# An encoder layer on one core: the first down phase is put in another order, and the output weights change queues

## The chip, the core and the metric

The kernel is one program on one core of a Trainium2 chip. The number that counts is the device time of the whole program in microseconds, median over several executions. The engines are called as the profile calls them: PE (TensorE, matrix products), PEld (its weight loads), DVE (VectorE), ACT (ScalarE), POOL (GpSimd) and SP (SyncE, which here does little but issue transfers). Each engine works through its own instructions in the order in which they are written. A transfer is issued by an engine, mostly SP, and an issue that has to wait holds up whatever stands behind it on that engine.

## The reference

One layer of a hybrid encoder runs over a prompt of 2048 rows and, with caches, over a sample of 32 rows. Cut to what matters:

```python
proj  = x @ w_in                                     # q, k, v, forget logits, gates, h
mixed = concat([attention(q, k, v, logf), gate_b * causal_conv(gate_c * h)]) @ w_out
x = layer_norm(ALPHA * x + mixed)
g, val = split(x @ w_up)                             # 2 x 2816 columns
a = silu(causal_conv(g)) * val
x = layer_norm(ALPHA * x + a @ w_down)               # 2816 -> 1024
```

The last product, `a @ w_down`, is where most of the change lies, and the one with `w_out` where the rest does.

## The kernel before

All large products are made of three matmuls (`three`, L89 to L91): each factor is split into a rounded high part (`hi`, L80 on ACT or L78 on POOL) and the rest (`lo`, L85, a subtraction on DVE), and high x high, high x low and low x high are added up in PSUM. So each 128x512 piece of a weight needs a transfer, an ACT cast and a DVE subtraction before PE can use it.

The program has these stages, by the times of the trace: input projections and attention to about 1083 us; the output projection `mix` with its LayerNorm to 1310; then, for the first half of the prompt rows together with the sample rows, the products with `w_up` (`up(0)`, to 1757) and with `w_down` (`down(0)`, to about 2015); then `up(1)` (to about 2447) and `down(1)` for the other half. The products of a phase follow Strassen's scheme with seven products in place of eight. In a down phase these are p2, p1, p5, p6, p3, p7, p4, in this order; each has 11 steps k = 0 to 10, and a step is 12 matmuls of 512 columns (four tiles times `three`), called d0 to d10 below.

**Weight parts.** A generator, `left()`, makes the parts of all weights in the order of the PE's steps. A raw weight is loaded by SP into a tile `wr` (four of them), then split into a part `wp` (a ring of nine; a step of a down phase takes two). `steps()` gives the order for a down phase: the list of `("d", g, p, k)`, with the 22 sample steps `("s", f)` put in between. A sample step multiplies a 128-row block of `w_down` with the sample's rows (four matmuls, `sample`, L1339). Its moving side is `sm`, split from one table `VM` that is written to memory row by row in the up phase (`vm<-row`) and loaded back once, before the first sample step, when the up phase has issued all its transfers (`gated`). Of a sample step's weight the second half's low part is made on POOL (L1086), the first half's on DVE.

**Weight sums.** Four of the seven products need sums of blocks of `w_down`. `weight_sums(x)` (L1215, 22 calls) loads four blocks into a tile `yx`, adds them on POOL and stores them to `TW` (`tw<-yx`) some steps later. There is one call at the end of each turn f = 1 to 22 of `up(0)`.

**The next factors.** While `down(0)` runs p1 and later products, `build()` makes the prompt factors of `up(1)`: for each of four k it loads a tile `r` (one buffer) and two tiles `q` (two buffers) from `XT`, makes four differences on POOL (L912) and seven splits (ACT and DVE, tiles `xb` and `xt`). `free(k)` advances it by one piece after each step.

**The output weights.** `fetch_out` loads `w_out` in eight blocks `wor` (two buffers). The first three are split by POOL and DVE (`wh`, `wl`) during the stage before and issued by SP. The other five are split by ACT and DVE (`woh`, `wol`), and their loads are issued by ACT. In `mix`, `load` brings the attention's result back: `m<-mxs` for the sample, then `m<-mx` for the first tiles of the prompt, all issued by ACT; POOL casts them (`ms`, `mh`) and DVE subtracts (`ms`, `ml`).

The order within each engine is the order of the written program, adjusted by a scheduler, so that where an instruction ends up is read from the compiled order.

Of the kernel before, what the change touches and what calls it, by code (L numbers as in the profile page):

```python
# [7 lines left out]
F32 = mybir.dt.float32  # L8
# [3 lines left out]
ALU = mybir.AluOpType  # L12
# [10 lines left out]
GT = 512  # L23
FF = 2816
NF = 22
# [36 lines left out]
class Kernel:  # L62
# [141 lines left out]
    def fetch_out(self, upto, tiles=None):  # L204

        for k in range(len(self.out), upto):
            r = self.wp.tile([128, 4, 264], F32, tag="wr", bufs=2, name="wor").rearrange("p a b -> p (a b)")[:, :DM]
            if tiles:
                a, b = tiles(k)
            else:  # L210
                a, b = (self.wp.tile([128, 1152], F32R, tag=t, bufs=3, name=t)[:, :DM] for t in ("wh", "wl"))
            self.dma(r, self.i["w_out"][128 * k:128 * k + 128], self.nc.scalar if tiles else None)
            self.hi(a, r, "act" if tiles else "pool")
            self.lo(b, r, a)
            self.out.append((a, b))
# [686 lines left out]
    def build(self):  # L902

        for k in range(4):
            r = self.fp.tile([128, 1060], F32, tag="z", bufs=1, name="r")[:, :2 * GT].rearrange("p (r c) -> p r c", r=2)
            q = [self.fp.tile([128, 4, 128], F32, tag="s", bufs=2, name="q").rearrange("p a b -> p (a b)")
                 for _ in range(2)]
            self.dma(r, self.XT[k])
            for x in range(2):
                self.dma(q[x], self.XT[k + 4][:, x])  # L910
            yield
            sub = lambda o, x, y: self.nc.gpsimd.tensor_tensor(out=o, in0=x, in1=y, op=ALU.subtract)  # L912
            b11, b12, b21, b22 = r[:, 0], r[:, 1], q[0], q[1]
            src = {"b11": b11, "b21": b21, "b22": b22, "t1": b11, "t3": b12, "t2": b22, "t4": b21}
            todo = {"t1": (b12, b11), "t3": (b22, b12), "t2": (b22, b11), "t4": (b21, b22)}
            for s in self.SETS:
                if s in todo:
                    sub(src[s], *todo[s])
                self.split([self.X[s][1][:, x, k] for x in range(2)], src[s])
                yield  # L920
# [4 lines left out]
    def steps(self, g):  # L925

        out = []
        sample = iter(range(NF if g == 0 else 0))
        for p in self.DOWN:
            for k in range(NK):  # L930
                out.append(("d", g, p, k))
                for _, f in list(zip(range((0, 3, 3, 3, 3, 2)[min(k, 5)]), sample)):
                    out.append(("s", f))
        return out

# [14 lines left out]
    def left(self):  # L950


        nc = self.nc
# [77 lines left out]
        for p, v in (("p1", a11), ("p2", a12)):  # L1031
            w = as_part(self.rp.tile([128, DM], F32R, tag="wr", bufs=4, name="w" + p))
# [10 lines left out]
        for g in range(2):  # L1043
            for f in range(NF + 1):
                todo = ["p1", "p6", "p5", "p2", "p7"] if f else ["p1", "p2", "p5", "p6", "p7"]
                if g == 0 and f == 0:
                    todo = todo[3:]
                elif f < NF:
                    while ("u", g, f) not in R:
                        yield  # L1050
                    yield 1
                    item(g, f, todo.pop(0))
                if f:
                    for p in ("p4", "p3"):
                        yield 1
                        item(g, f - 1, p)
                    R.pop(("u", g, f - 1))
                    S.pop((g, f - 1))
                    more(2)
                if f < NF:  # L1060
                    for p in todo:
                        yield 1
                        item(g, f, p)
            if g == 0:
                sm, self.gated = [], False
            for key in self.steps(g):
                if key[0] == "s" and not len(sm):

                    while not self.gated:
                        yield  # L1070
                    m = raw()[:, :NF * TS].rearrange("p (f c) -> p f c", f=NF)
                    self.dma(m, self.VM)
                    for q in range(2):
                        v = self.fp.tile([128, DM], F32R, tag="yx", bufs=2, name="sm")[:, :NK * 2 * TS]
                        v = v.rearrange("p (f x c) -> p f x c", f=NK, x=2)
                        self.split([v[:, :, 0], v[:, :, 1]], m[:, NK * q:NK * q + NK])
                        sm += [v[:, f] for f in range(NK)]
                yield 2
                r = R.pop(key)
                parts = []  # L1080
                for h in range(2):
                    v = part().rearrange("p x a b -> p x (a b)")
                    w = r[:, GT * h:GT * h + GT]
                    if key[0] == "s" and h:
                        self.hi(v[:, 0], w, "act")
                        nc.gpsimd.tensor_tensor(out=v[:, 1], in0=w, in1=v[:, 0].bitcast(F32), op=ALU.subtract)  # L1086
                    else:
                        self.split([v[:, 0], v[:, 1]], w)
                    parts.append(v)
                self.W[key] = (sm[key[1]], parts) if key[0] == "s" else parts  # L1090
                more(1)
# [9 lines left out]
    def up(self, g, eb, pp, starts=()):  # L1101
        nc = self.nc
# [148 lines left out]
        for f in range(NF + 1):  # L1251
            steps = []
            if f < NF:
                steps.append(lambda: p1(f))
            if f:
                steps += [lambda: p4(f - 1), lambda: p3(f - 1)]
            late = f == 0
            if f < NF:
                steps += [lambda: p2(f)] if late else [lambda: p6(f)]
            if f:  # L1260
                steps.append(lambda: taps(f - 1))
            if f < NF:
                steps.append(lambda: p5(f))
            if f:
                steps.append(lambda: gate(f - 1))
            if f < NF:
                steps += [lambda: p6(f)] if late else [lambda: p2(f)]
            if f:
                steps.append(lambda: close(f - 1))
            if f < NF:  # L1270
                steps.append(lambda: p7(f))
            for s in steps:
                s()
                if starts:
                    starts.pop(0)()
                for x in later:
                    x[0] -= 1
                for x in [x for x in later if not x[0]]:
                    later.remove(x)
                    x[1]()  # L1280
                self.refill()
            if g == 0 and 0 < f:
                weight_sums(f - 1)
        for x in later:
            x[1]()
        self.gated = True
# [5 lines left out]
    def down(self, g, sb, pp):  # L1292
        nc = self.nc
# [3 lines left out]
        y = {}  # L1297
# [45 lines left out]
        def product(p, s, start, each, head=0, tail=0):  # L1343
            if start:
                self.K[s] = banks()

            def add(q, k):
                v, w = self.W["d", g, p, k]
                qs = slice(128 * q, 128 * q + 128)
                self.three(self.K[s][q], v[:, 0, qs], v[:, 1, qs], w[:, 0], w[:, 1],  # L1350
                           start and k == 0, k == NK - 1, skip_group_check=not start)

            def free(k):
                self.W.pop(("d", g, p, k))
                self.held -= 2
                self.refill()
                work()
                if p != "p2":
                    next(build, None)

            for q in range(4):
                for k in range(head):
                    add(q, k)
            for k in range(NK - tail):
                if k >= head:
                    for q in range(4):
                        add(q, k)
                if k >= head - 1:
                    for x in range(head if k == head - 1 else 1):
                        free(k - (head - 1 - x) if k == head - 1 else k)  # L1370
                        if p == "p2" and g == 0:
                            while [w for w in self.W if w[0] == "s"]:
                                sample(min(w[1] for w in self.W if w[0] == "s"))
            for q in range(4):
                for k in range(NK - tail, NK):
                    add(q, k)
                if q == 3:
                    for k in range(NK - tail, NK):
                        free(k)
                each(q)  # L1380
# [243 lines left out]
```

## Time and profile before

| What | us |
|---|---|
| Median of three runs | 2678.01 (2675.28 to 2679.25) |
| The profiled execution | 2671.96 |
| Its span | 2670.1 |
| PE busy | 2557.1 |
| DVE busy | 1906.7 |
| ACT busy | 1121.1 |
| POOL busy | 665.0 |

The mean granted clock of TensorE in that execution is 0.986 of full speed. Times in rows are microseconds from the start of the span. In a list of groups a row names the line, the engine, the operation and the tiles (out<-in), the shape and the count; behind the first bar stand the busy time and the mean in ns, behind the second the engine's idle time ahead of these instructions and what ended most of it. In a list of waits a row gives the engine, its tile and line, what it waited for, the total, the number and the longest. In an engine's timeline a row gives start, duration, instruction and, in brackets, the idle time before it with what ended it; "SPq" and "ACTq" are transfers that SP and ACT issue, and the time is that of issuing. In windows each engine has its busy time and the count of instructions.

### The profile page before, as it was taken

How to read it: one execution, taken by the hardware profiler on the slowest of the kernel's cores; microseconds unless marked ns; L12 is line 12 of the kernel's file. 1: busy time of each engine (PE TensorE's matmuls, PEld its weight loads, DVE VectorE, ACT ScalarE, POOL GpSimd, SP SyncE). 2: the span in 40 equal slices, each digit the busy share in tenths (PEclk: the TensorE clock that was granted, in tenths of full speed). 3: DMA queues.
4: the chain of work that ended last, by engine and by line, in shares of the span. 5: the costliest groups of instructions: out<-in, count | busy, mean ns of one | idle time of the engine just before them, and what ended most of it. 6: DMA issues, size and time to landing. Idle time of an engine off the chain costs nothing. (4 is left out here: it accounts for less than half of the span.)

```text
span 2670.1 us, 41578 instructions
## 1 busy us (share of the span) xinstructions
PE 2557.1 (96%) x14802; PEld 2213.6 (83%) x14802; DVE 1906.7 (71%) x3610; ACT 1121.1 (42%) x2008; POOL 665.0 (25%) x589
## 2 busy tenths in 40 slices
PE   8999899999999999899999999979899999999998
PEld 8978688788887888688899999956788888888886
DVE  4466666767877777387777777757878877786658
ACT  2142443454544445132444444445544444444442
POOL 2234333232432242100024324343300111111000
PEclk9999899999999999899999999989999999999999
DMA  7777678668647643555534444478764232325765
GB/s 225 199 230 218 200 232 239 192 186 237 196 122 207 184 131 104 164 169 182 198 119 164 154 137 159 155 247 261 244 214 141 103 119 83 111 103 181 246 194 168
DMA packets 350776, 475.09 MB, mean 178 GB/s; under 512 B 42184, under 2 KB 221576, under 8 KB 350568
## 3 DMA queue, kind: packets, MB, share of 16 engines
q1 hardware_dynamic: 348520, 468.64, 56.2%
q10 hardware_dynamic: 2048, 3.80, 0.4%
q8 instruction: 116, 1.90, 0.3%
q14 instruction: 92, 0.75, 0.1%
HBM read 344.22 MB, written 128.11 MB: 177 GB/s over the span
## 5 line engine op out<-in xcount | busy, mean ns | idle before, releaser
L85 DVE TENSOR_TENSOR wp<-wr,wp 128x512 fp32r<-128x512 f32 x550 | 417.9, 781 | 155.8 <-ACT wp L80 151.9
L80 ACT CAST wp<-wr 128x512 fp32r<-128x512 f32 x572 | 339.3, 620 | 266.2 <-PE b L91 179.4
L89 PE MATMUL b<-xt,wp 128*128 128x264 f32 (+1 forms) x1056 | 338.3, 320 | 4.5 <-ACT row L1169 2.4
L90 PE MATMUL b<-xt,wp 128*128 128x264 f32 (+1 forms) x1056 | 337.3, 319 | 0.1
L91 PE MATMUL b<-xt,wp 128*128 128x264 f32 (+1 forms) x1056 | 337.4, 319 | 0.0
L89 PE MATMUL pm<-xh,wh 128*128 128x512 f32 (+1 forms) x800 | 289.5, 363 | 10.4 <-ACT xh L80 8.1
L90 PE MATMUL pm<-xl,wh 128*128 128x512 f32 (+1 forms) x800 | 285.1, 357 | 2.4 <-DVE xl L85 2.3
L91 PE MATMUL pm<-xh,wl 128*128 128x512 f32 (+1 forms) x800 | 284.5, 356 | 1.1 <-DVE wl L85 1.1
L525 POOL TENSOR_SCALAR p<-p,mx 128x128 f32<-128x128 f32 (+15 forms) x128 | 167.8, 1311 | 354.3 <-DVE mx L524 247.6
L89 PE MATMUL b<-xb,wp 128*128 128x264 f32 (+1 forms) x792 | 253.4, 320 | 0.0
L91 PE MATMUL b<-xb,wp 128*128 128x264 f32 (+1 forms) x792 | 253.0, 319 | 0.0
L90 PE MATMUL b<-xb,wp 128*128 128x264 f32 (+1 forms) x792 | 252.8, 319 | 0.0
L90 PE MATMUL b<-wp 128*128 128x512 f32 x616 | 242.7, 394 | 8.8 <-DVE wp L85 8.7
L89 PE MATMUL b<-wp 128*128 128x512 f32 x616 | 240.1, 392 | 4.7 <-ACT wp L80 3.5
L91 PE MATMUL b<-wp 128*128 128x512 f32 x616 | 240.7, 391 | 0.0
L523 ACT ACTIVATE p<-p,mx 128x128 f32<-128x128 f32 (+15 forms) x128 | 154.7, 1209 | 174.7 <-DVE mx L522 173.7
L89 PEld LDWEIGHTS b<-xt,wp 128*128 128x128 f32 x1056 | 198.9, 188 | 19.5 <-ACT row L1169 3.1
L90 PEld LDWEIGHTS b<-xt,wp 128*128 128x128 f32 x1056 | 198.8, 188 | 14.1 <-DVE xt L85 0.4
L91 PEld LDWEIGHTS b<-xt,wp 128*128 128x128 f32 x1056 | 199.0, 188 | 13.7
L1215 POOL TENSOR_TENSOR yx<-row 128x512 f32<-128x512 f32 x22 | 36.5, 1661 | 664.2 <-DVE row L1105 632.5
L89 PEld LDWEIGHTS pm<-xh,wh 128*128 128x128 f32 x800 | 153.5, 192 | 26.8 <-ACT xh L80 8.7
L85 DVE TENSOR_TENSOR wl<-wr,wh 128x1024 fp32r<-128x1024 f32 (+3 forms) x98 | 124.3, 1270 | 69.4 <-POOL wh L78 69.1
(297 smaller groups left out, 5914.3 us busy)
## 6 DMA issues: line engine op xcount, KB each, us to landing
wr<-in_w_mm SPq DMA_DIRECT2D x79, 512.0 KB
wr<-in_w_g SPq DMA_DIRECT2D x44, 512.0 KB
wr<-in_w_val SPq DMA_DIRECT2D x44, 512.0 KB
wr<-tw SPq DMA_DIRECT2D x88, 256.0 KB
k<-ks SPq DMA_DIRECT2D x80, 256.0 KB
vv<-vs SPq DMA_DIRECT2D x80, 256.0 KB
wr<-in_w_down SPq DMA_DIRECT2D x66, 256.0 KB
xr<-in_xt SPq DMA_DIRECT2D x48, 256.0 KB
```

The lines of the kernel that those rows point to most:

```text
L80: nc.scalar.copy(out, in_)
L85: self.nc.vector.tensor_tensor(out=out, in0=in_, in1=hi.bitcast(F32), op=ALU.subtract)
L89: mm(out, sh, mh, start=start, stop=False, **kw)
L90: mm(out, sh, ml, start=False, stop=False, **kw)
L91: mm(out, sl, mh, start=False, stop=stop, **kw)
L523: nc.scalar.activation(p, p, AF.Exp, bias=neg, accum_out=tot)
L525: nc.gpsimd.tensor_scalar(p, p, r, 1.0, op0=ALU.mult, op1=ALU.mult)
L1215: pool = lambda o, x, y, op: nc.gpsimd.tensor_tensor(out=o, in0=x, in1=y, op=op)
```

## The change

Six edits:

1. `fetch_out`: the five loads of `w_out` that ACT issued are issued by SP.
2. `build`: the four differences for each k are made on DVE.
3. `steps`: the 22 sample steps stand behind k = 5, 6, 7, 8, 9 of p2 (5, 5, 4, 4, 4) instead of from k = 1 on (3, 3, 3, 3, then 2 at a time).
4. `left`: the low part of the second half of a sample step's weight is made on DVE like the first half's.
5. `up`: two weight sums at f = 1 and at f = 11, one at the others, so that the last comes at f = 20 instead of 22.
6. `free`: `build` is advanced only after steps with even k.

```diff
-            self.dma(r, self.i["w_out"][128 * k:128 * k + 128], self.nc.scalar if tiles else None)
+            self.dma(r, self.i["w_out"][128 * k:128 * k + 128])
...
-            sub = lambda o, x, y: self.nc.gpsimd.tensor_tensor(out=o, in0=x, in1=y, op=ALU.subtract)
+            sub = lambda o, x, y: self.nc.vector.tensor_tensor(out=o, in0=x, in1=y, op=ALU.subtract)
...
             for k in range(NK):
                 out.append(("d", g, p, k))
-                for _, f in list(zip(range((0, 3, 3, 3, 3, 2)[min(k, 5)]), sample)):
+                for _, f in list(zip(range((5, 5, 4, 4, 4)[k - 5] if 5 <= k < 10 else 0), sample)):
                     out.append(("s", f))
...
                     v = part().rearrange("p x a b -> p x (a b)")
-                    w = r[:, GT * h:GT * h + GT]
-                    if key[0] == "s" and h:
-                        self.hi(v[:, 0], w, "act")
-                        nc.gpsimd.tensor_tensor(out=v[:, 1], in0=w, in1=v[:, 0].bitcast(F32), op=ALU.subtract)
-                    else:
-                        self.split([v[:, 0], v[:, 1]], w)
+                    self.split([v[:, 0], v[:, 1]], r[:, GT * h:GT * h + GT])
                     parts.append(v)
...
-            if g == 0 and 0 < f:
-                weight_sums(f - 1)
+            if g == 0:
+                for x in range(NF):
+                    if 1 + x * 20 // NF == f:
+                        weight_sums(x)
...
-                if p != "p2":
+                if p != "p2" and k % 2 == 0:
                     next(build, None)
```

Here is how the compiled order moves at three places. First the queue of ACT where the output projection begins; lines with a minus stand there before, lines with a plus now:

```order
 L609 COPY ot<-o3o 64x256
-L73 DMA wor<-in_w_out 128x1024 x2
 L73 DMA m<-mxs 128x8x32
 L73 DMA m<-mx_92 128x1024 x2
-L80 CAST woh<-wor 128x1024 x2
+L80 CAST woh<-wor 128x1024 x4
 L80 CAST wp_14509<-wr 128x512
-L73 DMA wor<-in_w_out 128x1024
 L80 CAST wp_14512<-wr 128x512
```

The three loads of the attention's result stand directly behind the last copy of the stage before. The first two loads of output weights now stand on SP, each behind a store of the attention's result:

```order
 L73 DMA fw<-in_fconv 128x88
 L73 DMA state<-in_sffn 128x44
-L73 DMA mx_95<-y 128x4x128 x2
+L73 DMA mx_95<-y 128x4x128
+L73 DMA wor<-in_w_out 128x1024
+L73 DMA mx_95<-y 128x4x128
+L73 DMA wor<-in_w_out 128x1024
 L73 DMA g_13258<-in_ln_g 128x1024
 L73 DMA b_13259<-in_ln_b 128x1024
```

Second, SP where the up phase ends and the table `VM` is loaded (`vb`, `va`, `vs`, `vd` are stores of the up phase's rows), before:

```order
L73 DMA vb_10_159<-row 128x1024
L73 DMA vm<-row 128x32
L73 DMA yx<-in_w_down 128x2x256 x2
L73 DMA va_10_158<-row 128x1024
L73 DMA vs_10_160<-yx 128x1024
L73 DMA vd_10_161<-row 512x1x128
L73 DMA tw_217<-yx 512x1x256
L73 DMA wr<-vm 128x704
L73 DMA wr<-in_w_down 128x1024 x3
L73 DMA wr<-vb_3_131 128x4x128
```

and now:

```order
L73 DMA vm<-row 128x32
L73 DMA vb_10_159<-row 128x1024
L73 DMA va_10_158<-row 128x1024
L73 DMA vs_10_160<-yx 128x1024
L73 DMA vd_10_161<-row 512x1x128
L73 DMA wr<-in_w_down 128x1024
L73 DMA wr<-vm 128x704
L73 DMA wr<-in_w_down 128x1024
L73 DMA wr<-vb_6_143 128x4x128
L73 DMA wr<-in_w_down 128x512
L73 DMA wr<-in_w_down 128x1024 x5
```

No weight sum stands ahead of the table's load any more, and the parts of d3 to d5 and four sample weights (`wr<-in_w_down 128x1024`) are loaded ahead of it; three of those four stand above these rows. Behind it come one sample step, d6, five sample steps, and so on, where before three sample steps and d3 came.

Third, DVE within p5, before (`r` and `q` come from POOL's differences):

```order
L85 TENSOR_TENSOR xb_13229<-r,xb_13229 128x512
L85 TENSOR_TENSOR wp<-wr,wp 128x512
L85 TENSOR_TENSOR xb_13230<-q,xb_13230 128x512
L85 TENSOR_TENSOR wp<-wr,wp 128x512 x2
L85 TENSOR_TENSOR xb_13231<-q,xb_13231 128x512
L85 TENSOR_TENSOR wp<-wr,wp 128x512
L85 TENSOR_TENSOR xt_13232<-r,xt_13232 128x512
```

and now:

```order
L85 TENSOR_TENSOR xb_13229<-r,xb_13229 128x512
L912 TENSOR_TENSOR r<-r 128x512
L85 TENSOR_TENSOR wp<-wr,wp 128x512 x2
L85 TENSOR_TENSOR xt_13232<-r,xt_13232 128x512
L85 TENSOR_TENSOR xb_13230<-q,xb_13230 128x512
L85 TENSOR_TENSOR wp<-wr,wp 128x512 x2
L85 TENSOR_TENSOR xb_13231<-q,xb_13231 128x512
L912 TENSOR_TENSOR r<-q,r 128x512
L912 TENSOR_TENSOR q<-q,r 128x512
L85 TENSOR_TENSOR wp<-wr,wp 128x512 x2
```

The differences stand between the weight parts on DVE itself, at most two weight parts ahead of the split that needs them.

## The prediction

> **What bounds the kernel now.** I read the page first, then the waits of PE, then three places in stretches of time.
>
> ```profile
> span 2670.1 us, 41578 instructions
> PE 2557.1 (96%) x14802; PEld 2213.6 (83%) x14802; DVE 1906.7 (71%) x3610; ACT 1121.1 (42%) x2008; POOL 665.0 (25%) x589
> ...
> PE bs L1339 <- DVE sm L85: 13.3, 1, 13.3
> PE b L90 <- DVE wp L85: 8.7, 10, 1.5
> PE mix L89 <- POOL ms L78: 7.1, 1, 7.1
> PE mix L89 <- POOL mh L78: 3.0, 2, 1.9
> PE b L89 <- ACT wp L80: 3.5, 3, 1.7
> ```
>
> TensorE is busy 96% of the span, so only its pauses and the halves of its clock can be won: 2670.1 - 2557.1 = 113 us in all. The edits touch three of them: the wait for `sm` (13.3), the waits for `ms` and `mh` (10.1), and part of those for weight parts `wp` (8.7 and 3.5).
>
> Place 1, the start of the output projection, in windows (columns: us, then PE, PEld, DVE, ACT, POOL busy with counts, granted clock, DMA share, GB/s), then what stood there on the queues of SP and ACT, on POOL, PE and DVE:
>
> ```profile
> 1080.00:1085.00 5.00, 3.09 (x14) 2.23 (x12) 2.83 (x3) 0.00 (x0) 2.09 (x2) 1.00 0.32 92
> 1085.00:1090.00 5.00, 0.00 (x0) 0.00 (x0) 0.31 (x1) 2.04 (x2) 0.28 (x1) 0.79 1.01 272
> 1095.00:1100.00 5.00, 3.95 (x9) 2.33 (x10) 3.53 (x4) 1.14 (x2) 1.04 (x1) 0.50 1.04 419
> 1105.00:1110.00 5.00, 5.00 (x23) 3.50 (x23) 1.68 (x2) 2.00 (x2) 0.00 (x0) 1.00 0.42 132
> ...
> 1078.40 5.82 SPq L73 DMA_DIRECT2D mx<-y  x2
> 1082.62 3.06 ACTq L73 DMA_DIRECT2D wor<-in_w_out  x2
> 1085.71 0.59 ACTq L73 DMA_DIRECT2D m<-mxs  x1
> 1087.58 1.04 ACT L80 CAST woh<-wor 128x1024 fp32r<-128x1024 f32 x1 [16.35 <-DMA mx<-y]
> 1089.72 0.40 POOL L78 TENSOR_SCALAR ms<-m 128x256 fp32r<-128x256 f32 x1 [5.67 <-DMA m<-mxs]
> 1090.18 0.64 PE L89 MATMUL mix<-wh,ms 128*32 128x512 f32 x1 [7.09 <-POOL ms L78]
> 1090.51 1.22 DVE L85 TENSOR_TENSOR wol<-wor,woh 128x1024 fp32r<-128x1024 f32 x1
> 1097.53 1.23 DVE L85 TENSOR_TENSOR ml<-m,mh 128x1024 fp32r<-128x1024 f32 x1 [1.47 <-POOL mh L78]
> 1099.00 0.63 PE L91 MATMUL mix<-wh,ml 128*128 128x512 f32 x1
> 1101.56 0.40 PE L89 MATMUL mix<-wh,mh 128*128 128x512 f32 x1
> ```
>
> PE leaves the stage before near 1083.1 (3.09 busy of the first five). The load of `m<-mxs` is issued only at 1085.71, behind two `w_out` loads on ACT's queue that stood there until 1082.62 and took 3.06 us more. PE's row names 7.09 us, POOL's cast 5.67 us of that transfer. The clock falls to 0.50 and is whole again from 1101.56 (0.40 us a row instead of 0.63).
>
> Place 2, the start of the first down phase:
>
> ```profile
> 1760.00:1770.00 10.00, 5.64 (x23) 3.67 (x21) 6.11 (x6) 2.71 (x5) 5.20 (x4) 1.00 0.43 138
> 1770.00:1780.00 10.00, 0.00 (x0) 0.00 (x0) 0.00 (x0) 0.15 (x1) 4.24 (x6) 0.53 0.83 290
> 1790.00:1800.00 10.00, 9.04 (x37) 5.08 (x37) 5.37 (x7) 6.31 (x12) 5.52 (x4) 1.00 0.86 283
> 1840.00:1850.00 10.00, 10.00 (x46) 8.29 (x45) 9.71 (x17) 7.82 (x14) 0.00 (x0) 1.00 0.97 315
> ...
> 1772.44 2.32 POOL L1215 TENSOR_TENSOR yx<-yx 128x256 f32<-128x256 f32 x3 [0.29 <-DMA yx<-in_w_down]
> 1774.79 0.57 SPq L73 DMA_DIRECT2D tw<-yx  x1
> 1775.45 0.58 SPq L73 DMA_DIRECT2D wr<-vm  x1
> 1776.08 1.94 SPq L73 DMA_DIRECT2D wr<-in_w_down  x3
> 1780.37 0.96 DVE L85 TENSOR_TENSOR sm<-wr,sm 128x352 fp32r<-128x352 f32 x2 [14.07 <-ACT sm L80]
> 1823.99 0.53 SPq L73 DMA_DIRECT2D wr<-vb  x1
> 1832.61 1.88 DVE L1325 TENSOR_TENSOR row<-b,row 128x512 f32<-128x512 f32 x3
> ```
>
> PE does nothing from 1770 to 1780. The table of sample rows (`wr<-vm`) is loaded behind the last weight sums: three POOL operations to 1774.76, their store at 1774.79, the load at 1775.45. A whole window holds 46 matmuls, 0.217 us each; from 1790 to 1830 there are 35 to 39, since the weights come slower than PE takes them.
>
> Place 3, products p1, p5 and p6, first the windows and DVE's groups there, then DVE's same group from 1925 to 2000, where POOL has nothing:
>
> ```profile
> 1832.40:1861.00 28.60, 27.39 (x120) 22.03 (x119) 25.82 (x41) 17.45 (x31) 8.79 (x4) 1.00 0.82 261
> 1861.00:1893.00 32.00, 29.79 (x130) 23.96 (x129) 26.65 (x40) 15.64 (x29) 6.48 (x4) 1.00 0.79 264
> 1893.00:1926.00 33.00, 28.13 (x112) 21.35 (x111) 30.50 (x40) 19.32 (x36) 14.46 (x8) 0.95 0.64 204
> ...
> L85 DVE TENSOR_TENSOR wp<-wr,wp 128x512 fp32r<-128x512 f32 x63 | 49.3, 823 | 1.8 <-ACT wp L80 1.7
> L85 DVE TENSOR_TENSOR xt<-r,xt 128x512 fp32r<-128x512 f32 x8 | 7.6, 953 | 3.6 <-ACT xt L80 3.6
> L85 DVE TENSOR_TENSOR wp<-wr,wp 128x512 fp32r<-128x512 f32 x56 | 36.5, 686 | 17.0 <-ACT wp L80 17.0
> ...
> 1862.81 3.70 DVE L85 TENSOR_TENSOR wp<-wr,wp 128x512 fp32r<-128x512 f32 x6
> 1850.16 2.52 POOL L912 TENSOR_TENSOR r<-r 128x512 f32<-128x512 f32 x1 [20.92 <-DVE xb L85]
> ```
>
> PE pauses 93.6 - 85.3 = 8.3 us here. DVE is busy 83.0 us of the 93.6, and its subtractions take longer beside POOL's: 823 ns against 686. Alone, they follow each other every 0.60 us (six end 3.70 us after they start).
>
> **The change, part by part, against the profiled execution's 2671.96 us.**
>
> *Output weights on SP's queue.* Five loads leave ACT's queue, so `m<-mxs` need not stand behind two of them. Its other waits are for stores that SP issues ahead of 1078.40, so it can go out by then; POOL cast it 4.0 us after the issue (1089.72 - 1085.71), now it has to let the running cast of `wh` end first, so `ms` is there at about 1084.3, a good 1 us after PE is free. PE's six sample matmuls follow at once, but `ml` stands behind the first `wol` on DVE in both orders. The first `wor` load now follows the first of the two stores at 1078.40 on SP and still waits for its buffer, so it goes out at about 1082.6; `woh`, which ended 6.0 us after that issue (1087.58 + 1.04 - 1082.62), ends near 1088.6; then 1.2 us each for `wol` and the first `ml`: 1091.0. PE's first matmul on `ml` is at 1099.00 now, so 8 us are won; PE still pauses some 3 us ahead of it, and the half clock after 1099.00 was worth (1101.56 - 1099.00) / 2 = 1.3 us, which may or may not be saved. I take 7.5, bounds 4 (if `wor` lands later beside the `m` loads) and 10 (the two named waits). SP's own loads for the next stage stand behind the moved ones, with over 200 us of PE work in between: nothing.
>
> *Weight sums ended by f = 20, sample steps after k = 5 to 9.* Two turns of the up phase get two sums instead of one; POOL, busy 25% of the span, takes under 1 us an operation (three in 2.32 us): nothing, at worst 1 us where a store of rows stands behind them. At the start of p2 PE now has d0 to d5, 72 matmuls, 16 us, before it needs `sm`: it works from 1757.6 to about 1774 instead of stopping near 1765. On SP the last `tw` store and its sums are gone, so `wr<-vm` goes out earlier by the three sums and the store, 2.32 + 0.57, at 1772.5; `sm` follows, as now, 5.9 us behind it (1780.37 + 0.96 - 1775.45), near 1778.5. PE's pause is 5 us instead of 15. But PE is not all: behind 1775.45 SP issues 26 steps until 1823.99, 1.84 us each; in the new order 22 are left behind `vm`, from 1773.1: the last goes out at 1773.1 + 22 x 1.84 = 1813.6, 10.4 us sooner. PE's work from 1778.5, 148 matmuls x 0.217 = 32 us, would end at 1811, so supply still decides. The sample's second halves no longer pass POOL beside DVE, which shortens a step a little: I take 11, bounds 6 (each early sample load waits for a buffer held until PE takes its part) and 15 (the whole difference of the pauses plus the shorter steps).
>
> *Subtractions of the build on DVE, over twice the steps.* Added to DVE: 16 x 0.60 = 9.6 us. Taken from it: 63 x (823 - 686) + 8 x (953 - 686) ns = 10.8 us. So DVE's load stays at 82 us, for 396 matmuls x 0.217 = 86 us of PE work. What falls away are the stops for the transfers of `r` and `q` and for POOL's results; the twice longer spacing gives a transfer two steps of 2.6 us more. I take 5 of the 8.3 us, bounds 0 (DVE, at 95%, is itself the limit) and 8.
>
> Sum: 7.5 + 11 + 5 = 23.5, from 4 + 6 + 0 = 10 to 10 + 15 + 8 = 33. That is 2648.5 us in the profiled execution's time. The median of the runs, 2678.01, lies 6.05 above that execution, so I predict **2654.5**.
>
> The Trainium skill, page "DMA: Bandwidth & Descriptors", section "Issuing engines are not separate DMA queues", says that starting transfers from several engines saves only the issuing time. By it, moving five loads between queues would be worth nothing; the rows of place 1 speak otherwise, as the load there waited not for a transfer but behind two loads that waited for buffers.
>
> **The rivals.**
>
> *The order of the queues is worth nothing.* The `m` loads and the `w_out` loads share the transfer engines, 1.01 to 1.04 of their time from 1085 to 1100. If the same bytes only come in another order, PE waits for `ml` as long as now. For it: that share. Against it: `m<-mxs` could go when the share was 0.32 or less. Then 11 + 5 = 16, so 2662. Chance 0.12. The rule just named would make it this.
>
> *The sample's part comes at the pace of its weights wherever it stands.* For it: 283 GB/s and a share of 0.86 in p2, against 315 and 0.97 at the most. If the steps loaded ahead only fill buffers and PE catches up with the supply, p2 ends where it did: 7.5 + 5 = 12.5, so 2665.5. Chance 0.12. Against it: the supply itself starts 2.4 us earlier and with four sample steps behind it.
>
> *DVE becomes the limit in p1, p5 and p6, and the kernel slower.* DVE now has, in order, a subtraction, then the part that needs ACT's cast of it, with PE's weight parts behind. If a subtraction there costs with its waits what POOL's cost, 2.52 us for the first, DVE needs 83.0 - 10.8 + 16 x 2.52 = 112.5 us, and with the stops for transfers that it has now (10.6, 93.6 - 83.0) 123 us against 93.6: 29.5 lost, 18.5 won elsewhere, so 2678 + 11 = 2689. It turns slower than before from 1.9 us each, and shows as slower from 2.2. For it: DVE at 82 of 86 us even in the good case. Against it: 0.60 us alone, and ACT busy only 52 of the 93.6 us. Chance 0.06.
>
> **How the numbers follow.** The forecast with all three gains has 0.70 and its own range 2645 to 2668; the first two rivals 0.24, inside 2655 to 2672; the third 0.06. The range that holds 8 of 10: 2643 to 2669. What a measurement here can tell from no change is 0.2%, 5.4 us. All of the forecast but a sliver, and most of the first two rivals, are faster; a mix of both rivals and a loss in place 3 gives no change. Faster 0.87, same 0.07, slower 0.06.
>
> **What would show it.** Right: PE's wait for `ms` gone from its list, and a first `ml` matmul some 8 us earlier after the stage before; `wr<-vm` within about 15 us of the first p2 matmul and a pause of 4 to 7 us there; p2 about 64 us long instead of 75; no POOL rows between p2 and p6, the mean of DVE's `wp` near 690 ns there, and p1, p5 and p6 in about 88.5 us. Wrong: the same waits under another name, DVE's `wp` as the releaser of PE at many steps, or the supply of p2 at 1.84 us a step from a later start.

## The result and the profile after

The changed kernel takes 2645.72 us (median of three runs, 2644.67 to 2645.92) against 2678.01. The ratio of the runs is 0.9896, with a 95% interval of 0.9878 to 0.9915: faster by 1.0%. The forecast was 2654.5, with a range from 2643 to 2669. The profiled execution has a span of 2644.0 us, 26.1 less than before.

The page and the waits of PE, after:

```profile
span 2644.0 us, 41534 instructions
PE 2548.9 (96%) x14802; PEld 2211.7 (84%) x14802; DVE 1915.4 (72%) x3648; ACT 1121.7 (42%) x2008; POOL 610.1 (23%) x551
...
PE bs L1336 <- DVE sm L85: 7.8, 1, 7.8
PE b L89 <- ACT wp L80: 4.1, 3, 2.3
PE b L90 <- DVE wp L85: 2.7, 2, 1.9
PE mix L89 <- POOL ms L78: 1.4, 1, 1.4
```

The waits for `ms` fell from 7.1 to 1.4, those for `sm` from 13.3 to 7.8, those for DVE's parts of weights (L90) from 8.7 to 2.7. The same engine stays the bound.

Three places of the trace. First the start of the output projection, after (windows; then ACT's queue, POOL and PE):

```profile
1085.00:1090.00 5.00, 3.36 (x9) 1.63 (x10) 2.60 (x3) 1.05 (x1) 3.14 (x2) 0.73 0.83 275
1095.00:1100.00 5.00, 5.00 (x24) 3.62 (x23) 0.00 (x0) 0.21 (x1) 0.00 (x0) 1.00 0.97 360
...
1077.64 0.59 ACTq L73 DMA_DIRECT2D m<-mxs  x1
1084.59 0.40 POOL L78 TENSOR_SCALAR ms<-m 128x256 fp32r<-128x256 f32 x1
1092.06 0.50 PE L91 MATMUL mix<-wh,ml 128*128 128x512 f32 x1 [0.70 <-DVE ml L85]
1083.27 0.39 PE L91 MATMUL pm<-xh,wl 128*128 128x512 f32 x1
```

The load of `m<-mxs` is issued at 1077.64 instead of 1085.71. From the last matmul of the stage before (1083.27) to the first on `ml` (1092.06) it is 8.8 us, where it was 16.3 (the last matmul before is at 1082.70), and PE is full with a whole clock from 1095 on.

Second, the start of p2, after:

```profile
1749.53 0.28 PE L91 MATMUL b<-xb,wp 128*128 128x264 f32 x1
1757.88 2.99 POOL L1210 TENSOR_TENSOR yx<-row 128x512 f32<-128x512 f32 x1 [29.49 <-DVE row L1100]
1757.93 0.32 SPq L73 DMA_DIRECT2D vm<-row  x1
1764.34 1.60 POOL L1210 TENSOR_TENSOR row<-row,yx 128x512 f32<-128x512 f32 x1
1765.97 0.56 SPq L73 DMA_DIRECT2D vd<-row  x1
1767.30 0.40 SPq L73 DMA_DIRECT2D wr<-vm  x1
1773.04 9.86 PE L1336 MATMUL bs<-wp,sm 128*64 128x512 f32 x33 [7.81 <-DVE sm L85]
1808.22 0.52 SPq L73 DMA_DIRECT2D wr<-vb  x1
1816.38 2.48 DVE L1322 TENSOR_TENSOR row<-b,row 128x512 f32<-128x512 f32 x4
```

And what answers to three of these rows in the kernel before, with the end of `up(0)` first:

```profile
1757.45 0.28 PE L91 MATMUL b<-xb,wp 128*128 128x264 f32 x1
1766.28 1.29 POOL L1215 TENSOR_TENSOR yx<-row 128x512 f32<-128x512 f32 x1 [2.36 <-DVE row L1105]
1766.64 0.38 SPq L73 DMA_DIRECT2D vm<-row  x1
1771.50 0.57 SPq L73 DMA_DIRECT2D vd<-row  x1
```

Counted from the end of `up(0)`, the sample's table is loaded as late as before: 1767.30 - 1749.53 = 17.8 us, before 1775.45 - 1757.45 = 18.0. The weight sums are gone from SP, but POOL's four sums of rows now take 8.0 us (`vm` to `vd`) where they took 4.9: their first operation lasts 2.99 us instead of 1.29. p2, from the end of `up(0)` to DVE's first row after it, takes 66.9 us instead of 75.2.

Third, p1, p5 and p6, after (windows, then DVE's group of weight parts from the end of p2 to the end of p6):

```profile
1850.00:1860.00 10.00, 10.00 (x46) 8.28 (x45) 8.35 (x14) 3.42 (x6) 0.00 (x0) 1.00 0.89 297
1880.00:1890.00 10.00, 10.00 (x46) 8.28 (x45) 10.00 (x18) 5.67 (x11) 0.00 (x0) 1.00 0.66 204
1900.00:1910.00 10.00, 10.00 (x45) 8.26 (x44) 10.00 (x17) 7.17 (x13) 0.00 (x0) 1.00 0.72 231
...
L85 DVE TENSOR_TENSOR wp<-wr,wp 128x512 fp32r<-128x512 f32 x71 | 45.3, 680 | 1.0 <-ACT wp L80 1.0
```

PE is full in these windows, although DVE is too in two of them, and the mean of `wp` is 680 ns instead of 823. The end of p3 shows the sum: 1937.46 - 1816.38 = 121.1 us behind the end of p2, before 1964.65 - 1832.61 = 132.0:

```profile
1937.46 2.48 DVE L1322 TENSOR_TENSOR row<-b,row 128x512 f32<-128x512 f32 x4
```

### The profile page after: what moved, and what is told of

The parts are those of the page before. It is cut to its first block, busy times and chain, and to the rows that moved or that the text cites. A ratio compares the mean times of both kernels' runs of the same rounds, so it can differ in the third digit from the quotient of the medians.

```text
span 2644.0 us, 41534 instructions
## 1 busy us (share of the span) xinstructions
PE 2548.9 (96%) x14802; PEld 2211.7 (84%) x14802; DVE 1915.4 (72%) x3648; ACT 1121.7 (42%) x2008; POOL 610.1 (23%) x551
## 4 chain that ended last, share of the span: by engine, by line
PE 66%; DVE 5%; DMA 4%; issue 4%; ACT 1%; POOL 1%; SPq 0%; POOLq 0%; DVEq 0%; ACTq 0%
PE b L89 15%; PE b L91 15%; PE b L90 15%; PE pm L89 2%; PE pm L90 2%; PE pm L91 2%; PE o3o L605 2%; PE pt3t L581 2%; PE mix L91 1%; DMA wr<-in_w_down 1%; PE mix L89 1%; PE mix L90 1%; PE o2o L605 1%; DMA xr<-in_xt 1%; PE pt2t L581 1%
## 5 line engine op out<-in xcount | busy, mean ns | idle before, releaser
L90 PE MATMUL b<-xt,wp 128*128 128x264 f32 (+1 forms) x1056 | 337.0, 319 | 0.3 <-DVE xt L85 0.3
L90 PE MATMUL pm<-xl,wh 128*128 128x512 f32 (+1 forms) x800 | 284.7, 356 | 2.3 <-DVE xl L85 2.3
L90 PE MATMUL b<-xb,wp 128*128 128x264 f32 (+1 forms) x792 | 252.8, 319 | 0.0
L90 PE MATMUL b<-wp 128*128 128x512 f32 x616 | 240.3, 390 | 2.7 <-DVE wp L85 2.7
L90 PEld LDWEIGHTS b<-xt,wp 128*128 128x128 f32 x1056 | 198.6, 188 | 14.4 <-DVE xt L85 0.5
```

Source lines behind the costliest of these rows:

```text
L90: mm(out, sh, ml, start=False, stop=False, **kw)
```

## How the runs are compared

The same attention stage ends between 1070.0 and 1083.9 us in the profiled executions below, in kernels that do not differ there. Whole times of single executions therefore scatter by several us. The stages behind it hardly scatter, so each experiment is read by stage, from five points of its trace: the last matmul of the attention stage (`pm`), the last of `up(0)`, DVE's first row behind p2, its first row behind p3, and the end of the span.

| kernel | projection and up(0) | p2 | p1 to p3 | rest | sum | median of its runs |
|---|---|---|---|---|---|---|
| before | 674.8 | 75.2 | 132.0 | 705.4 | 1587.4 | 2678.0 |
| changed | 666.3 | 66.9 | 121.1 | 706.5 | 1560.7 | 2645.7 |
| changed, again | 666.3 | 65.8 | 121.1 | 707.8 | 1561.0 | 2644.0 |
| output weights back on ACT | 674.4 | 65.8 | 121.1 | 705.1 | 1566.4 | 2655.4 |
| differences back on POOL | 667.6 | 65.8 | 131.6 | 705.4 | 1570.4 | 2653.3 |
| build after every step | 668.2 | 66.2 | 121.1 | 705.4 | 1560.9 | 2643.0 |
| samples early | 667.5 | 69.6 | 121.1 | 705.4 | 1563.5 | 2642.6 |
| sample's low part back on POOL | 667.5 | 68.7 | 121.1 | 706.4 | 1563.8 | 2642.7 |
| weight sums up to f = 22 | 666.4 | 70.0 | 121.1 | 705.5 | 1563.0 | 2645.5 |
| last sums on DVE | 666.3 | 62.9 | 121.1 | 705.4 | 1555.7 | 2639.1 |
| table early, stores by POOL | 666.6 | 66.7 | 121.1 | 705.8 | 1560.1 | 2640.7 |
| last sums on DVE, samples later | 667.7 | 63.4 | 121.1 | 705.3 | 1557.5 | 2638.8 |

The changed kernel's 26.7 us are 8.5 + 8.3 + 11.0 - 1.1, in the order of the columns. Each row is one profiled execution. In the kernels that change nothing in p2 that stage still scatters, from 65.8 to 66.9 us, so that the gain in p2 is 8.3 to 9.4 us. In the kernels with edit 1 the first column lies between 666.3 and 668.2, the rest between 705.3 and 707.8, and p1 to p3, where nothing of it is changed, agrees within 0.1. The two experiments that are not in the table are told at their place. The kernel before was run again beside these; its medians there were 2675.5, 2671.6 and 2669.3 us.

## The experiments

**The output weights back on ACT.**

```diff
-            self.dma(r, self.i["w_out"][128 * k:128 * k + 128])
+            self.dma(r, self.i["w_out"][128 * k:128 * k + 128], self.nc.scalar if tiles else None)
```

> The changed kernel with edit 1 undone: the five loads of w_out are issued by ACT again. Theory (the m loads stood behind loads that waited for buffers): the wait for ms comes back at about 7 us, the first matmul on ml stands some 15.9 us behind the last matmul of the stage before, as in the kernel before, instead of 8.8 us, the clock is at half speed to about 18 us behind it, and the time is 7 to 9 us over the changed kernel's, about 2653. Rival (the order of the queues is worth nothing, the other edits gave the gain): within 2 us of the changed kernel.

The wait is back, and with it 8.1 us of this stage and no other; the ratio to the kernel before is 0.9929 (0.9909 to 0.9949). By the medians it is 9.6 us over the changed kernel, where 7 to 9 were expected.

```profile
PE mix L89 <- POOL ms L78: 7.1, 1, 7.1
PE mix L89 <- POOL mh L78: 3.3, 2, 2.3
...
1098.86 0.63 PE L91 MATMUL mix<-wh,ml 128*128 128x512 f32 x1
```

The last matmul ahead of the projection is at 1082.14 there, so the first on `ml` is 16.7 us behind it (in the kernel before it was 16.3, not the 15.9 of the expectation). Edit 1 alone thus accounts for 8.1 of the 8.5 us. The Trainium skill, page "DMA: Bandwidth & Descriptors", section "Issuing engines are not separate DMA queues", puts the worth of another issuing engine at the issuing time alone. The 8.1 us measured here are more than that: the loads on ACT waited for buffers, and what stood behind them waited too.

**The differences back on POOL, at the wide spacing; and the narrow spacing, with the differences on DVE.**

```diff
-            sub = lambda o, x, y: self.nc.vector.tensor_tensor(out=o, in0=x, in1=y, op=ALU.subtract)
+            sub = lambda o, x, y: self.nc.gpsimd.tensor_tensor(out=o, in0=x, in1=y, op=ALU.subtract)
```

> The changed kernel with edit 2 undone: the build's differences are on POOL again, still spread over twice the steps. Theory (POOL's additions hold up DVE's subtractions): DVE's wp mean in p1, p5 and p6 rises from 680 to about 800 ns, PE loses 4 to 9 us there, the time is about 2650 to 2655. Rival (the twice longer spacing alone gave the gain, since the transfers of r and q then have time): the mean rises, but PE loses under 2 us.

```diff
-                if p != "p2" and k % 2 == 0:
+                if p != "p2":
                     next(build, None)
```

> The changed kernel with edit 6 undone: differences on DVE, the build advanced after every step. Theory (POOL was the cause): within 2 us of the changed kernel. Rival (the spacing is the cause): PE loses 4 to 9 us in p1, p5 and p6, as DVE waits in order for r and q, and the time is 2650 to 2655.

These two tell edit 2 and edit 6 apart, and all of the gain is edit 2's: 131.6 us from p2 to p3 with POOL, 121.1 with DVE at either spacing. The 10.5 us lost with POOL are more than the 4 to 9 expected. DVE's group with POOL at work, and the ends of p2 and p3 of that run:

```profile
L85 DVE TENSOR_TENSOR wp<-wr,wp 128x512 fp32r<-128x512 f32 x60 | 48.3, 840 | 2.4 <-ACT wp L80 2.1
...
1811.28 2.48 DVE L1322 TENSOR_TENSOR row<-b,row 128x512 f32<-128x512 f32 x4
1942.88 2.48 DVE L1322 TENSOR_TENSOR row<-b,row 128x512 f32<-128x512 f32 x4
```

The ratios to the kernel before are 0.9925 (0.9906 to 0.9944) and 0.9881 (0.9863 to 0.99). The rival that the transfers of `r` and `q` needed the spacing has fallen.

**Work on POOL that nothing waits for.** What POOL costs could be its holding up DVE, or the way from POOL's result through ACT to DVE. This kernel keeps the differences on DVE and adds POOL work beside them (`idle` is a tile of 96 columns):

```diff
                     sub(src[s], *todo[s])
+                    for n in range(5):
+                        v = src[s][:, 96 * n:96 * n + 96]
+                        self.nc.gpsimd.tensor_tensor(out=self.idle, in0=v, in1=v, op=ALU.subtract)
```

> The changed kernel with work on POOL that nothing waits for but the next load into the same tile: behind each of the build's 16 differences on DVE, POOL reads its result in five subtractions of 96 columns. From the end of p2 to the end of p3 it takes 121.1 us in the changed kernel, 131.6 with the differences on POOL and 132.0 in the kernel before. Theory (what is lost is DVE's time, held up by any addition on POOL that reads): the mean of DVE's wp rises from 680 ns to 740 or more and the stretch takes 124 to 130 us. Rival (what is lost is the way DVE, ACT and DVE again wait for POOL's result): 121 to 122 us.

```profile
L85 DVE TENSOR_TENSOR wp<-wr,wp 128x512 fp32r<-128x512 f32 x65 | 45.7, 738 | 0.5 <-ACT wp L80 0.3
...
L921 POOL TENSOR_TENSOR idle<-q 128x96 f32<-128x96 f32 x40 | 27.9, 698 | 8.5 <-DVE q L912 5.4
```

DVE's mean rises from 680 to 738 ns and p1 to p3 from 121.1 to 125.3 us: work on POOL alone, of which no product needs a result, costs 4.2 us. PE's waits for weight parts in this stretch are 3.4 us, against 0.8 in the changed kernel; its full windows hold 46 matmuls in 10 us in both. (This POOL work also holds its tile against the next load, so a part of the 4.2 can be that.) The 10.5 us with the differences on POOL are not reproduced in full, since 80 small operations are not 16 large ones; how the rest divides into DVE's longer instructions and the way over ACT is open. In the Trainium skill, page "SBUF — State Buffer", section "Who interferes with whom", DVE and GpSimd share a pair of ports under an exclusive lock. The lengths here fit that, though no run shows the lock itself: 680 ns alone, 738 and 840 beside POOL, and POOL's own sum 2.99 us beside DVE against 1.29 with DVE at rest.

**The samples early again.**

```diff
-                for _, f in list(zip(range((5, 5, 4, 4, 4)[k - 5] if 5 <= k < 10 else 0), sample)):
+                for _, f in list(zip(range((0, 3, 3, 3, 3, 2)[min(k, 5)]), sample)):
```

> The changed kernel with edit 3 undone: sample steps from k = 1 of p2 on again, the other edits kept. If the pause ahead of the first sample step sets the end of p2: the pause grows from 7.8 to about 13 us or more, and p2 ends 5 us or more later. If the supply of weights sets it: the pause grows as much, but p2 ends within 2 us of the changed kernel, since the table is loaded as early and the same number of weights follows it.

```profile
1752.38 0.38 SPq L73 DMA_DIRECT2D vm<-row  x1
1757.23 0.52 SPq L73 DMA_DIRECT2D vd<-row  x1
1757.85 0.58 SPq L73 DMA_DIRECT2D wr<-vm  x1
1762.42 7.99 PE L1336 MATMUL bs<-wp,sm 128*64 128x512 f32 x24 [9.00 <-DVE sm L85]
1803.91 0.52 SPq L73 DMA_DIRECT2D wr<-vb  x1
1813.24 2.48 DVE L1322 TENSOR_TENSOR row<-b,row 128x512 f32<-128x512 f32 x4
```

Neither expectation was right on the pause: it grew to 9.0 us only, because the table now came at 14.2 us behind the end of `up(0)` (1743.67) instead of 17.8. With the samples early DVE has no parts of d3 to d5 to make while POOL adds, and POOL's sums take 4.9 us from `vm` to `vd`, as in the kernel before: each of the four lasts 1.26 to 1.29 us. p2 takes 69.6 us, 2.7 to 3.8 more than the changed kernel and 5.6 less than the kernel before. So edit 3 is worth some 3 us of p2's 8.3; it takes back through POOL what it could have won at the table.

**The sample's low part back on POOL, and the weight sums up to f = 22.**

```diff
-                    self.split([v[:, 0], v[:, 1]], r[:, GT * h:GT * h + GT])
+                    w = r[:, GT * h:GT * h + GT]
+                    if key[0] == "s" and h:
+                        self.hi(v[:, 0], w, "act")
+                        nc.gpsimd.tensor_tensor(out=v[:, 1], in0=w, in1=v[:, 0].bitcast(F32), op=ALU.subtract)
+                    else:
+                        self.split([v[:, 0], v[:, 1]], w)
```

> The changed kernel with edit 4 undone: the low part of the second half of a sample weight is made on POOL again. From the end of up(0) to the end of p2 it takes 66.9 us in the changed kernel and 75.2 in the kernel before. Theory (in p2 a step is paced by its transfer, cast and subtraction, and the one on POOL is the slowest and holds up DVE's): p2 takes 69 to 72 us. Rival (the pace is the transfers' alone): within 1 us of 66.9.

```diff
-            if g == 0:
-                for x in range(NF):
-                    if 1 + x * 20 // NF == f:
-                        weight_sums(x)
+            if g == 0 and 0 < f:
+                weight_sums(f - 1)
```

> The changed kernel with edit 5 undone: weight sums at the end of every turn up to f = 22. Theory (three sums and a store stand ahead of the table's load): the load is issued 3 to 4 us later than the 17.8 us behind the end of up(0) in the changed kernel, the pause ahead of the samples grows from 7.8 to about 11, and p2 takes 2 to 4 us more. Rival (the supply decides): the pause grows, p2 stays within 1 us of 66.9.

The first takes 68.7 us for p2, a little under the theory's 69 and over what the rival allows, by 0.8; that is 1.8 to 2.9 us more than the changed kernel. PE's list names `POOL wp` for 3.5 us, but 1.3 us of the loss are a longer pause (9.1 us): the table's load went out 0.9 us later. How much the pace of the steps gave is therefore not settled. In the second the table's load goes out at 1757.22, 20.9 us behind the end of `up(0)` (1736.37), and the pause grows by 3.8 us and p2 by 3.1 to 4.2, as the theory said:

```profile
1763.74 9.81 PE L1334 MATMUL bs<-wp,sm 128*64 128x512 f32 x33 [11.63 <-DVE sm L85]
```

The ratios are 0.9898 (0.9875 to 0.9921) and 0.9902 (0.987 to 0.9934): by whole times neither can be told from the changed kernel. By p2, each undone alone, edits 3, 4 and 5 are worth about 3, 2 and 3 us.

**Half the bytes of the samples' weights.**

```diff
-                self.dma(r, self.i["w_down"][128 * f:128 * f + 128])
+                self.dma(r[:, :GT], self.i["w_down"][128 * f:128 * f + 128, :GT])
...
-                    self.split([v[:, 0], v[:, 1]], r[:, GT * h:GT * h + GT])
+                    self.split([v[:, 0], v[:, 1]], r[:, :GT] if key[0] == "s" else r[:, GT * h:GT * h + GT])
```

> The changed kernel where each sample step loads only the first half of its weight's columns (256 KB instead of 512) and makes both of its parts from it, so that the sample's second half of columns is not computed; casts, subtractions and matmuls stay in number. If the transfers set the pace of p2 behind the pause: 22 times 256 KB less at the 300 GB/s seen there is 19 us less transfer, and p2 falls from 66.9 us to what casts, subtractions and PE leave, 57 to 60 us. If ACT and DVE set it: 65 us or more.

In its one execution p2 takes 61.3 us, 4.5 to 5.6 less, between the two expectations. 1.9 of these are a shorter pause (5.9 us). The transfers were busy 87% of the rest of p2 in the changed kernel and are 72% busy here, so bytes are a part of the pace of p2, but halving the samples' share of them wins at most 5.6 us, where the expectation put the transfer time saved at 19.

**What is left of the pause.** The last four sums of `up(0)` on DVE:

```diff
-            pool(s1, a21, a22, ALU.add)
+            op = add if g == 0 and k == NK - 1 else pool
+            op(s1, a21, a22, ALU.add)
...
```

> The changed kernel with the four sums of the last pair of rows in up(0) made on DVE. In the changed kernel these stand on POOL beside DVE's subtractions and take 8.0 us from the store of the last sample rows to the store of the last sums, 4.9 in the kernel before, where DVE stood still. Theory (POOL and DVE hold each other up, and the table's load stands behind it): under 5.5 us, the table's load 2.5 us or more earlier, the pause about 5 instead of 7.8 and p2 1 to 3 us shorter. Rival (the stores, not the sums, take the time): no change.

```profile
1758.59 0.32 SPq L73 DMA_DIRECT2D vm<-row  x1
1763.40 0.56 SPq L73 DMA_DIRECT2D vd<-row  x1
1764.07 0.79 SPq L73 DMA_DIRECT2D wr<-vm  x1
1771.02 9.36 PE L1337 MATMUL bs<-wp,sm 128*64 128x512 f32 x32 [5.08 <-DVE sm L85]
```

From `vm` to `vd` it is 4.8 us, the table is loaded 13.9 us behind the end of `up(0)` (1750.19), the pause is 5.1 us and p2 62.9: the theory held, and p2 gained 2.9 to 4.0 us, rather more than the 1 to 3 expected. By stages this is the best of the kernels that compute everything, 5.0 us under the changed one, 3.9 of them in p2 and 1.2 in the rest, which it does not touch; its ratio to the kernel before is 0.9876 (0.9848 to 0.9905).

Two further versions won nothing on top. In the first, POOL issues the last stores itself, and the table has a buffer of its own (`by` is POOL's queue for the last pair of rows; the stores of `a` and `d` change in the same way):

```diff
-            after(3, lambda: self.dma(c, ss))
+            after(3, lambda: self.dma(c, ss, by))
...
+            self.rows = eb.tile([128, 1060], F32, tag="z", bufs=1, name="vmt")[:, :NF * TS].rearrange("p (f c) -> p f c", f=NF)
+            self.dma(self.rows, self.VM)
```

> The changed kernel with the last three stores of the sums issued by POOL instead of SP, and the sample table loaded into a buffer of its own right behind the store of its last rows. Theory (SP stands behind POOL's sums for 8 us, with the table and the weights behind it): the table's load is issued about 9 to 10 us behind the end of up(0) instead of 17.8, the pause falls from 7.8 to 0 to 2 us, and p2 takes 4 to 8 us less than 66.9. If the supply decides alone: SP's weights start earlier too, so p2 gains as well; if the table's tiles wait for the sums in any case, the pause stays over 4 us.

```profile
1750.39 0.32 SPq L73 DMA_DIRECT2D vmt<-vm  x1
1757.42 3.42 PE L1339 MATMUL bs<-wp,sm 128*64 128x512 f32 x14 [2.69 <-DVE sm L85]
1762.48 0.48 ACT L80 CAST sm<-vmt 128x352 fp32r<-128x352 f32 x1 [7.53 <-DMA vs<-yx]
...
PE bs L1339 <- ACT wp L80: 5.1, 6, 2.7
```

The load went out at 11.4 us and the pause fell to 2.7, but PE then waited 5.1 us for the samples' parts from ACT, and p2 stayed at 66.7. The expected 4 to 8 us did not come. The row of ACT shows why: the table got a buffer of its own, but `sm` is still made in a tile that it shares with the sums (`yx`, two buffers). ACT cast the first half of `sm` and then stood 7.5 us at the second half, until the store of the sums (`vs<-yx`) had landed, with the samples' weight parts behind it. So the wait was moved rather than removed, and this run does not tell what p2 would take without it.

In the second, the sample steps come one step later on top of the sums on DVE:

```diff
-                for _, f in list(zip(range((5, 5, 4, 4, 4)[k - 5] if 5 <= k < 10 else 0), sample)):
+                for _, f in list(zip(range((6, 6, 5, 5)[k - 6] if 6 <= k < 10 else 0), sample)):
```

> The changed kernel with the last four sums of up(0) on DVE, as in the experiment before, and the sample steps one step later still (6, 6, 5, 5 behind k = 6 to 9 of p2). If the pause is what is left to win: PE has 12 more matmuls, 2.6 us, before the samples, the pause falls from 5.1 to about 2.5 us, and p2 from 62.9 to about 60.5. If the supply decides by now: p2 stays at 62 to 64. Against the changed kernel 4 to 6 us less.

p2 takes 63.4 us, as the case of the supply had it; the load of the table went out 1.4 us later (15.3), and the pause is 4.65. The changed kernel was run beside it:

> The changed kernel itself, beside the one above on the same chip: from the last matmul ahead of the output projection to the end of the program it should take 1560.7 us again, within 1 us, whatever the stage ahead of it takes.

It gave 1561.0 us, 0.3 off. Over six runs each, the ratios to the kernel before are 0.989 (0.9868 to 0.9912) for the version and 0.9904 (0.9886 to 0.9922) for the changed kernel. The intervals overlap, so the whole time does not show that the version beats it; by stages p2 is 2.4 to 3.5 us shorter.

## Why the prediction was right, and where it was not

The total fell into the stated range, but with luck: p2 was priced 2.7 us too high and the third place 6.0 too low, and these misses partly cancel.

**The output projection** was priced at 7.5 us and gave 8.5. The chain of the prediction stands in the trace link by link: `m<-mxs` out before 1078.4, `ms` near 1084.6, then `ml` behind the first `wol`. The first matmul on `ml` was put at 1091.0 and came at 1092.06, with an attention stage that ended 0.6 us later. PE's matmuls were slow, 0.63 us each, from 1087.29 to 1090.71 only, instead of from 1090.18 to 1101.56, so the clock was at half speed for some 3 us instead of 11. PE's wait for `ms`, which was to be gone, still shows 1.4 us. The rival that the order of the queues is worth nothing has fallen.

**p2** was priced at 11 and gave 8.3 (9.3 in the changed kernel's second profile). The step that failed is "`wr<-vm` goes out earlier by the three sums and the store", 2.9 us: it went out 0.2 us earlier, at 17.8 us behind the end of `up(0)` instead of 15.0. The sums and the store were gone, as said, but edit 3 put DVE's work on d3 to d5 beside POOL's four sums, which took 3.2 us longer (8.04 against 4.86 from `vm` to `vd`), and a weight load stood ahead of the table. The prediction knew the price of DVE beside POOL, but did not ask what these four sums now stood beside. The pause came out at 7.8 us for that reason, not at 5. The pace was right: 22 steps went out from 1767.80 to 1808.22, 1.84 us each, and 2.8 us of start is what the term was off. The experiment with the sums on DVE gives it back: 62.9 us, 12.2 under the kernel before. The forecast put the gain down to PE's early work and the missing sums; by the runs it is about 3 us for the samples' place, 3 for the weight sums and 2 for the low parts.

**p1, p5 and p6** were priced at 5, with bounds of 0 and 8, and gave 11.0, beyond the upper bound. POOL as the cause was right. The step that failed is the size: 5 of 8.3 us of pauses, held down because DVE at 82 of 86 us "is itself the limit". It is not; PE is full with DVE at 8 to 10 of 10. And 8.3 was not all there was, since busy time counts slow matmuls too: the clock was at 0.87 from 1910 to 1920. The prediction took 396 matmuls of 0.217 us for this stretch, 46 to a window of 10 us. A window also counts those that began before it; the starts themselves lie 0.227 us apart, as two matmuls of the kernel before with eleven between them show:

```profile
1840.11 0.39 PE L89 MATMUL b<-wp 128*128 128x512 f32 x1
1842.83 0.39 PE L89 MATMUL b<-wp 128*128 128x512 f32 x1
```

And by its own three windows the stretch holds at most 120 + 130 + 112 = 362 matmuls. At 0.227 us these are 82 us of the 93.6, so that some 11 us could be won. They were: from 1926 to the end of p3 PE waits for nothing in the kernel before, and in the changed kernel it waits 0.8 us from p1 to p3. There the 528 matmuls of the four products take 528 x 0.227 = 119.9 of the 121.1 us, which is why the stretch is so constant. "The twice longer spacing" was named as a part of the gain and is worth nothing. The third rival, DVE as the limit, has fallen: a difference on DVE has a mean of 0.69 us, and the stops for its operands did not reach PE. (By the prediction's own sum the kernel would have turned slower from 1.83 us each, not 1.9.)

**The total** was 8.8 us too high. 3.2 of it are the terms (23.5 against 26.7 by stages). The other 5.6 come from the 6.05 us added between the profiled execution and the median, as if they were a property of the kernel. They look like scatter: the changed kernel's profiled execution and its median are both 2645.7, and the kernel before had medians of 2669.3 to 2678.0 in four sets of runs.

**The rival on the supply** was half right: p2 is paced at 1.84 us a step with transfers busy 87%, but p2 did end earlier.

## What to carry to other kernels

In this kernel an issue that waited for a buffer held everything behind it on its engine, so the question about a queue is what stands behind a load that has to wait. The same holds for a buffer that is shared: the early table won nothing where `sm` still waited for a tile of the sums. When a step is moved forward, ask what it now runs beside: here it moved DVE's work beside POOL's and gave back at one end what another edit had won. Compare stages, not whole spans, when a stage outside the change scatters by more than the effect.

## What was not expected of the hardware

The attention stage ended between 1070.0 and 1083.9 us in fourteen profiled executions, while the stretch from p2 to p3 came out at 121.1 us in eleven of the twelve that have the differences on DVE, the other being the one with added work on POOL.

In that one, the matmuls of `up(1)` ran 1.8% further apart than in the changed kernel, at a granted clock of 1.00: 435 in 100 us against 443, first that run, then the changed kernel's second profile:

```profile
2100.00:2200.00 100.00, 100.00 (x435) 81.39 (x434) 73.35 (x101) 44.56 (x68) 12.61 (x8) 1.00 0.25 90
```

```profile
2100.00:2200.00 100.00, 100.00 (x443) 82.84 (x442) 75.00 (x101) 45.12 (x69) 12.61 (x8) 1.00 0.25 90
```

Why is open; for that reason only its stretch from p2 to p3 was used.
